# Two heads of a recurrence on opposite halves of the partitions, with PSUM tiles of their own

## The chip, the cores and the metric

The kernel runs on one core of a Trainium2 chip. The metric is the device time of the core in microseconds. The median of three runs of the kernel before is 3598.74 us (3598.61 to 3620.54).

## The reference

Two layers of a decoder trunk run on a prompt of 1024 positions and on 8 samples of 4 positions, at width 1024. One projection of the normalised input feeds two branches: a linear recurrence of 8 heads (RWKV-7) and a sliding-window attention. Their outputs are gated and merged, and a convolutional feed-forward block follows. All inputs are float32. The change concerns the recurrence, which per head keeps a 64x64 state:

```
def step(S, inp):
    r_t, w_t, k_t, v_t, kk_t, a_t = inp
    sk = jnp.einsum('bhvk,bhk->bhv', S, kk_t)
    S = (S * w_t[:, :, None, :]
         - sk[..., None] * (kk_t * a_t)[:, :, None, :]
         + v_t[..., None] * k_t[:, :, None, :])
    return S, jnp.einsum('bhvk,bhk->bhv', S, r_t)
S_T, y = lax.scan(step, wkv0, (r, w, k, v, kk, a))
```

## The kernel before

**Stages.** A layer first projects its input and prepares the operands of the recurrence (`rw_proj`, `rw_elem`), then runs the recurrence, then attention, merge and feed-forward. The loop over positions is replaced by chunks of 64 positions, 16 chunks in all; two chunks are a segment, so there are 8 segments a layer. The 8 heads stand in 4 pairs (`hp`), and in a pair head h=0 uses partitions 0 to 63 of the operands and h=1 partitions 64 to 127 (`hs[h]`).

**A segment.** `rw_elem` computes psL (L532) per head, already in the stage before. `m_front` loads BK, RA and VV, computes psG (L575; two halves q, per half four matmuls for each head, evicted by VectorE into GB), scales BK on GpSimd (L580), transposes it to psT (L585), which ScalarE copies to Bt (L586), and transposes VV to psV (L589), which ScalarE copies to the upper half of UV (L591). `m_inv` inverts the 32x32 blocks by 62 VectorE operations and a trip through HBM into Tt. `m_comb` joins two 32x32 blocks to one of 64 by three groups of 16 matmuls or transposes of 32x32 (L628, L631, L634) with a ScalarE copy behind each.

**A chunk.** `m_chain` does the dependent steps for each chunk c. x: `xb` collects GB·UV for each head (L658) and RA·S for each pair (L663 to L665), where the state S of a pair is a block-diagonal 128x128. VectorE copies the upper half to X (L670). u: `ub` gets Tt·X per head (L673), and ScalarE writes its negative to the lower half of UV (L674). sb: Bt·UV per head (L677), added on VectorE to the decayed state SW (L683; SW comes from GpSimd, L669). y: GB·UV into the lower half of `xb` (L685), copied by ScalarE to Y (L688). `m_post` normalises Y and transposes it (psY, L820); `m_sample` does the same recurrence for the samples in small pieces (psS L760, psSn L786).

**Fill.** Behind the steps, `fill` issues matmuls of an independent projection (psg, L373 to L375, float32r, 352 columns), from a generator that goes on in later stages. HK says how many portions go behind each step of a chunk. A portion is two groups of three matmuls.

**Order and pools.** The order of the instructions on each engine is made by a scheduler that looks at dependencies and at free buffers; only the place of the fill is pinned (behind the last matmul of a step). PSUM has 8 banks: one for fill (`pd`), four for psG, psT, psV, comb, psY and the samples (`pg`, tag g), and three for the chain (xb, ub, sb).

Attention, in a later stage, has one place that the prediction looks at: psQ, where for eight sequences the program issues a matmul with 128 moving columns (L891) and one with 32 (L892) in turn, each pair on the next of four column quarters.

Of the kernel before, what the change touches and what calls it, by code (L numbers as in the profile page):

```python
# [60 lines left out]
KC = {}  # L61
# [67 lines left out]
class Trunk:  # L129
# [299 lines left out]
    def rw_elem(self, l, hp, sg, zz):  # L429
# [97 lines left out]
        gm = self.cst("gmask", 64, p=64, o=64).unsqueeze(1).to_broadcast([64, 4, 64])  # L527
        for h in range(2):
            hs = slice(64 * h, 64 * h + 64)
            ps = self.pg.tile([64, 4, 64], F32, name="psL", tag="g")  # L530
            for c in range(4):
                self.lastL = nc.tensor.matmul(ps[:, c, :], BK[hs, 128 * c:128 * c + 64], RA[hs, 128 * c + 64:128 * c + 128], start=True, stop=True)  # L532
            V.tensor_tensor(Lm[:, :, h, :], ps, gm, ALU.mult)
# [12 lines left out]
    def m_state(self):  # L546
        nc, rw = self.nc, self.rw
        self.st = [rw.tile([128, 4, 128], F32, name=f"st{i}") for i in range(2)]
        self.X = rw.tile([128, 4, 128], F32, name="X")
        for t in self.st:  # L550
            nc.gpsimd.memset(t, 0.0)

    def m_front(self, l, sg):
# [13 lines left out]
        gm = self.cst("gmask", 128).unsqueeze(1).to_broadcast([128, 4, 128])  # L567
        for q in range(2):
            for h in range(2):
                hs = slice(64 * h, 64 * h + 64)  # L570
                ps = self.pg.tile([128, 4, 128], F32, name="psG", tag="g")
                for i in range(4):
                    hp, c = 2 * q + i // 2, i % 2
                    cs = slice(128 * c, 128 * c + 128)
                    nc.tensor.matmul(ps[:, i, :], BK[hs, hp, cs], RA[hs, hp, cs], start=True, stop=True)  # L575
                V.tensor_tensor(GB[:, 2 * q:2 * q + 2, :, h, :].rearrange("p a c t -> p (a c) t"), ps, gm, ALU.mult)
# [4 lines left out]
        for q in range(2):  # L581
            pt = self.pg.tile([128, 4, 128], F32, name="psT", tag="g")
            for i in range(4):
                hp, c = 2 * q + i // 2, i % 2
                nc.tensor.transpose(pt[:, i, :], BW[:, hp, c], ident)  # L585
            A.copy(Bt[:, 2 * q:2 * q + 2].rearrange("p a c t -> p (a c) t"), pt)  # L586
# [3 lines left out]
        for c in range(2):  # L590
            A.copy(UV[64:128, :, c, :], pv[64 * c:64 * c + 64])  # L591
        return dict(RA=RA, GB=GB, Bt=Bt, UV=UV)

    def m_inv(self, l, sg):
# [19 lines left out]
        for b in range(2):  # L614
            q[IQ[1]].dma_start(Tt[64 + 32 * b:96 + 32 * b, :, 32 * b:32 * b + 32],
                              rd[:, 16 * b:16 * b + 16])
        return Tt

    def m_comb(self, l, sg, m, Tt):
        nc, rw = self.nc, self.rw  # L620
        A, GB = nc.scalar, m["GB"]
        m["Tt"] = Tt
        TB = rw.tile([128, 16, 32], F32, name="TB", tag="TB")
        G = GB.rearrange("p a c h t -> p (a c h) t")
        pt = self.pg.tile([128, 16, 32], F32, name="psT1", tag="g")
        p1, p2, p3 = pt[0:32], pt[96:128], pt[64:96]
        for u in range(16):
            nc.tensor.transpose(p1[:, u, :], Tt[64:96, u, 0:32], self.con[64:96, KC["ident"] + 64:KC["ident"] + 96])  # L628
        A.copy(TB[0:32], p1)
        for u in range(16):  # L630
            nc.tensor.matmul(p2[:, u, :], G[0:32, u, 96:128], TB[0:32, u, :], start=True, stop=True)  # L631
        A.copy(TB[96:128], p2)
        for u in range(16):
            nc.tensor.matmul(p3[:, u, :], TB[96:128, u, :], Tt[96:128, u, 32:64], start=True, stop=True)  # L634
        A.activation(Tt[64:96, :, 32:64], p3, AF.Copy, scale=-1.0)

    def m_chain(self, l, sg, m):
# [6 lines left out]
        for c in range(2):  # L644
# [3 lines left out]
            xb = self.px.tile([128, 4, 128], F32, name="xb", tag="x", bufs=PM[2])  # L648
            ub = self.px.tile([64, 4, 128], F32, name="ub", tag="u")
            sb = self.px.tile([128, 4, 64], F32, name="sb", tag="s")  # L650
            X = self.X
            for hp, h in ph:
                last = first and hp == 3 and h == 1
                if last:
                    nc.tensor.matmul(xb[0:64, hp, hs[h]], GB[64:128, hp, c, h, 0:64], UV[64:128, hp, c, hs[h]], start=False, stop=False)
                    mm = nc.tensor.matmul(xb[64:128, hp, hs[h]], GB[64:128, hp, c, h, 64:128], UV[64:128, hp, c, hs[h]], start=False, stop=True)
                else:
                    nc.tensor.matmul(xb[:, hp, hs[h]], GB[64:128, hp, c, h, :], UV[64:128, hp, c, hs[h]],  # L658
                                     start=hp == h == 0, stop=False)
            if not first:  # L660
                r = 128 * c
                for hp in range(3):
                    nc.tensor.matmul(xb[:, hp, :], RA[:, hp, r:r + 128], S0[:, hp, :], start=False, stop=False)  # L663
                nc.tensor.matmul(xb[64:128, 3, :], RA[:, 3, r + 64:r + 128], S0[:, 3, :], start=False, stop=True)
                mm = nc.tensor.matmul(xb[0:64, 3, :], RA[:, 3, r:r + 64], S0[:, 3, :], start=False, stop=False)  # L665
            if not first:
                SW = rw.tile([128, 4, 64], F32, name="SW", tag="SW")
                for h in range(2):
                    P.tensor_tensor(SW[hs[h]], S0[hs[h], :, hs[h]], self.wc[hs[h], :, n:n + 1].to_broadcast([64, 4, 64]), ALU.mult)  # L669
            V.tensor_copy(X[64:128], xb[64:128])  # L670
            self.fill(HK[0], mm)
            for hp, h in ph:
                mm = nc.tensor.matmul(ub[:, hp, hs[h]], Tt[64:128, 4 * hp + 2 * c + h, :], X[64:128, hp, hs[h]], start=True, stop=True)  # L673
            A.activation(UV[0:64, :, c, :], ub, AF.Copy, scale=-1.0)  # L674
            self.fill(HK[1], mm)
            for hp, h in ph:
                mm = nc.tensor.matmul(sb[hs[h], hp, :], Bt[:, hp, c, hs[h]], UV[:, hp, c, hs[h]], start=True, stop=True)  # L677
            for h in range(2):
                s1 = S1[hs[h], :, hs[h]]
                if first:  # L680
                    V.tensor_copy(s1, sb[hs[h]])
                else:
                    V.tensor_tensor(s1, sb[hs[h]], SW[hs[h]], ALU.add)  # L683
            for hp, h in ph:
                mm = nc.tensor.matmul(xb[0:64, hp, hs[h]], GB[0:64, hp, c, h, 0:64], UV[0:64, hp, c, hs[h]],  # L685
                                 start=False, stop=hp == 3 and h == 1)
            self.lastM = mm
            A.copy(Y[64 * c:64 * c + 64], xb[0:64])  # L688
            self.fill(HK[2], mm)
        if sg == 7:  # L690
            for h in range(2):
                nc.sync.dma_start(self.a["o_pwkv"][l, :, 64 * h:64 * h + 64, :].rearrange("a k v -> k a v"), S1[hs[h], :, hs[h]])
# [51 lines left out]
    def m_sample(self, l, S):  # L744
# [6 lines left out]
        X = self.X[0:64]  # L751
# [419 lines left out]
    def run(self):  # L1171
# [42 lines left out]
        for l in range(self.layers):  # L1214
# [8 lines left out]
            self.tt = [self.iv.tile([128, 16, 64], F32, name=f"Tt{i}") for i in range(2)]  # L1223
# [165 lines left out]
```

## Time and profile before

| | |
|---|---|
| median of three runs | 3598.74 us |
| profiled execution, first to last instruction | 3583.3 us |
| TensorE busy | 3505.3 us, 98% |
| VectorE, ScalarE, GpSimd busy | 56%, 30%, 25% |
| DMA, mean busy share of the queue's engines | 30.7% |
| recurrence of layer 0, from 300 to 615 us | 302.56 of 315 us TensorE busy, granted clock 0.91 |
| recurrence of layer 1, from 2069 to 2412 us | 331.45 of 343 us TensorE busy, granted clock 0.88 |

The profile is one execution on the chip. The span runs from the first to the last instruction. A matmul of float32 operands appears as two passes, one of float32r operands or a transpose as one. The ends of matmuls are modelled and overlap the start of what follows, so the cost of a stretch of matmuls is the time from its first start to the first start behind it. "64*64" behind a matmul is the part of the array it uses (rows that are contracted, by columns). Of the granted clock, 1.00 is 2.4 GHz and 0.50 is 1.2 GHz.

### The profile page before, as it was taken

The page shows a single profiled execution, that of the slowest core. Times are in us where ns is not written, and L with a number is a line of the kernel's source. Part 1 is how long each engine was busy: PE and PEld are TensorE (multiplying, and loading weights), DVE is VectorE, ACT ScalarE, POOL GpSimd, SP SyncE. Part 2 cuts the span into 40 slices and gives each one's busy share as a digit, 9 for nine tenths or more (in the row PEclk, how much of TensorE's full clock was granted, in tenths as well). Part 3 has the DMA queues.
Part 4 walks back from the last instruction along what each step waited for, and adds up shares of the span by engine and source line. Part 5 has one row for each costly group of instructions (what it writes and reads, how often), then busy time and mean ns, then how long its engine had stood idle before and what let it go on. Part 6 is the DMA issues. An engine that isn't in the chain of part 4 may idle for free. (4 is left out here: it accounts for less than half of the span.)

```text
span 3583.3 us, 60195 instructions
## 1 busy us (share of the span) xinstructions
PE 3505.3 (98%) x24022; PEld 3316.4 (93%) x24022; DVE 2019.3 (56%) x4177; ACT 1081.4 (30%) x1854; POOL 879.5 (25%) x1070
## 2 busy tenths in 40 slices
PE   8999999999999999999999999999999999999998
PEld 7998887888999999999999988878889999999998
DVE  5767775564545445445557767746644544544445
ACT  4442222354331222112334422223533212212222
POOL 5541122131221111111346312212212211111112
PEclk9999998999999999999999989889999999999999
DMA  3345442525531111111223444325265311111111
GB/s 124 103 125 151 114 108 78 190 73 184 194 127 49 42 48 49 40 48 49 69 93 114 129 126 123 98 73 192 73 206 176 115 43 48 49 46 42 48 39 69
DMA packets 268920, 346.32 MB, mean 97 GB/s; under 512 B 82064, under 2 KB 213136, under 8 KB 268352
## 3 DMA queue, kind: packets, MB, share of 16 engines
q1 hardware_dynamic: 267488, 342.21, 30.7%
q8 instruction: 189, 3.10, 0.4%
q14 instruction: 91, 0.75, 0.1%
q10 hardware_dynamic: 1152, 0.26, 0.0%
HBM read 246.16 MB, written 98.25 MB: 96 GB/s over the span
## 5 line engine op out<-in xcount | busy, mean ns | idle before, releaser
L223 PE MATMUL psd<-lo,wh 128*128 128x352 f32 (+1 forms) x4368 | 1413.5, 324 | 3.9 <-DVE lo L244 3.9
L222 PE MATMUL psd<-hi,wh 128*128 128x352 f32 (+1 forms) x4368 | 1401.5, 326 | 11.0 <-DVE z L280 4.6
L224 PE MATMUL psd<-hi,wl 128*128 128x352 f32 (+1 forms) x4368 | 1405.8, 324 | 0.0
L222 PEld LDWEIGHTS psd<-hi,wh 128*128 128x128 f32 x4368 | 819.0, 188 | 16.4 <-ACT hi L243 4.1
L223 PEld LDWEIGHTS psd<-lo,wh 128*128 128x128 f32 x4368 | 824.8, 189 | 7.8 <-DVE lo L244 5.9
L224 PEld LDWEIGHTS psd<-hi,wl 128*128 128x128 f32 x4368 | 821.2, 188 | 1.9 <-DVE lo L244 0.2
L214 ACT CAST wh<-wr 128x1024 fp32r<-128x1024 f32 (+2 forms) x364 | 269.5, 742 | 1232.9 <-PE psd L223 894.5
L373 PE MATMUL psg<-hi,wh 128*128 128x352 f32 x1056 | 373.1, 353 | 24.5 <-DVE gt L379 22.7
L374 PE MATMUL psg<-lo,wh 128*128 128x352 f32 x1056 | 355.3, 336 | 0.0
L375 PE MATMUL psg<-hi,wl 128*128 128x352 f32 x1056 | 355.0, 336 | 0.0
L1105 DVE TENSOR_TENSOR xa<-xa,psd 128x352 f32<-128x352 f32 x456 | 226.9, 518 | 122.6 <-PE psd L224 111.2
L280 DVE TENSOR_TENSOR cz<-psd,rs 128x352 f32<-128x352 f32 (+2 forms) x176 | 72.1, 431 | 340.3 <-PE psd L224 339.7
L1078 POOL COPY cpo<-cz 128x2 f32<-128x2 f32 x44 | 8.1, 185 | 1024.4 <-DVE cz L280 1024.4
L215 DVE TENSOR_TENSOR wl<-wr,wh 128x256 fp32r<-128x256 f32 (+2 forms) x293 | 224.0, 767 | 55.6 <-ACT wh L214 55.3
L373 PEld LDWEIGHTS psg<-hi,wh 128*128 128x128 f32 x1056 | 207.5, 196 | 46.0 <-DVE gt L379 27.8
L375 PEld LDWEIGHTS psg<-hi,wl 128*128 128x128 f32 x1056 | 207.4, 196 | 5.1 <-issue 3.4
L374 PEld LDWEIGHTS psg<-lo,wh 128*128 128x128 f32 x1056 | 208.5, 197 | 2.3 <-issue 0.5
L1086 DVE SCALAR_TENSOR_TENSOR ct<-cz,prm,ct 128x1024 f32<-128x1024 f32 x88 | 159.1, 1808 | 62.8 <-ACT ct L1083 60.2
L215 POOL TENSOR_TENSOR wl<-wr,wh 128x1024 fp32r<-128x1024 f32 x71 | 171.3, 2413 | 39.8 <-ACT wh L214 38.3
L1093 DVE TENSOR_TENSOR ct<-psd,ct 128x352 f32<-128x352 f32 x132 | 64.9, 521 | 192.0 <-POOL ct L1089 154.7
L608 DVE TENSOR_TENSOR it<-R,Lt 128x60 f32<-128x60 f32 (+24 forms) x496 | 133.9, 270 | 26.6 <-POOL R L603 13.5
L610 DVE TENSOR_TENSOR R<-R,it 128x60 f32<-128x60 f32 (+24 forms) x496 | 129.9, 262 | 12.0
(314 smaller groups left out, 4511.0 us busy)
## 6 DMA issues: line engine op xcount, KB each, us to landing
wr<-wff SPq DMA_DIRECT2D x88, 512.0 KB
wr<-win SPq DMA_DIRECT2D x72, 512.0 KB
wr<-wdn SPq DMA_DIRECT2D x152, 128.0 KB
td<-gt SPq DMA_DIRECT2D x96, 176.0 KB
gl<-td SPq DMA_DIRECT2D x32, 528.0 KB
ox<-od SPq DMA_DIRECT2D x16, 528.0 KB
rt<-td SPq DMA_DIRECT2D x48, 176.0 KB
td<-rt SPq DMA_DIRECT2D x48, 176.0 KB
```

Source lines behind the costliest of these rows:

```text
L214: nc.scalar.copy(wh, wr)
L215: (sub or nc.vector).tensor_tensor(wl, wr, wh.bitcast(F32), ALU.subtract)
L222: self.nc.tensor.matmul(ps, wh, xh[:, s], start=i == 0, stop=False)
L223: self.nc.tensor.matmul(ps, wh, xl[:, s], start=False, stop=False)
L224: self.nc.tensor.matmul(ps, wl, xh[:, s], start=False, stop=i == last)
L373: nc.tensor.matmul(ps, wh[:, k], hi[:, s], start=k == 0, stop=False)
L374: nc.tensor.matmul(ps, wh[:, k], lo[:, s], start=False, stop=False)
L375: nc.tensor.matmul(ps, wl[:, k], hi[:, s], start=False, stop=k == 7)
L608: V.tensor_tensor(tv, R[:, 0:c, j:j + 1].to_broadcast([128, c, i]), Lt[:, j:j + 1, j + 1:32].to_broadcast([128, c, i]), ALU.mult)
L610: V.tensor_tensor(R[:, 0:c, j + 1:32], R[:, 0:c, j + 1:32], tv, ALU.subtract)
L1086: V.scalar_tensor_tensor(t[:, 0:TP], z[:, i:i + TP], w[i], t[:, 0:TP], ALU.mult, ALU.add)
L1105: V.tensor_tensor(x[:, s], x[:, s], ps, ALU.add)
```

## The change

The second head of each pair is mirrored: for h=0 V and X and T stand in partitions 64 to 127 and U in 0 to 63, as before; for h=1 it is the other way round. So the two heads of a pair contract over different halves of the array's rows. Each head has a PSUM tile of its own, and the program writes the matmuls of the two heads alternately.

- psL: one PSUM tile per head, heads alternate.
- psG: each 128-column matmul becomes two of 64 columns, so that h=1 lands mirrored; twice as many matmuls, on four positions of the array.
- Bt, UV: ScalarE's copies are cut by head, 3 for Bt per half instead of 1, 4 for UV per segment instead of 2.
- comb: one PSUM tile, one TB and three ScalarE operations for each head.
- m_chain: xb and ub become one tile per head, x and u side by side in one bank; the state is 128x4x64 instead of block-diagonal 128x4x128; RA·S is 16 matmuls of 64x64 for a chunk instead of 5 for whole pairs; X copies, the negation of u and the copy of Y are done per head; the state's addition and SW are one operation instead of two.
- Tt is loaded by 4 DMAs a segment instead of 2; the memset of the states goes.

The core of the diff:

```diff
+        psL = [self.pg.tile([64, 4, 64], F32, name=f"psL{h}", tag="g") for h in range(2)]
+        for c in range(4):
+            for h in range(2):
+                self.lastL = nc.tensor.matmul(psL[h][:, c, :], BK[hs[h], 128 * c:128 * c + 64],
+                                              RA[hs[h], 128 * c + 64:128 * c + 128], start=True, stop=True)
         for h in range(2):
-            for c in range(4):
-                self.lastL = nc.tensor.matmul(ps[:, c, :], BK[hs, 128 * c:128 * c + 64], RA[hs, 128 * c + 64:128 * c + 128], start=True, stop=True)
...
         for q in range(2):
+            ps = [self.pg.tile([128, 4, 128], F32, name=f"psG{h}", tag="g") for h in range(2)]
+            for i in range(4):
+                hp, c = 2 * q + i // 2, i % 2
+                for e in range(2):
+                    cs = slice(128 * c + 64 * e, 128 * c + 64 * e + 64)
+                    for h in range(2):
+                        nc.tensor.matmul(ps[h][hs[h ^ e], i, :], BK[hs[h], hp, cs], RA[hs[h], hp, 128 * c:128 * c + 128],
+                                         start=True, stop=True)
...
-            A.copy(Bt[:, 2 * q:2 * q + 2].rearrange("p a c t -> p (a c) t"), pt)
+            bt = Bt[:, 2 * q:2 * q + 2].rearrange("p a c t -> p (a c) t")
+            A.copy(bt[:, :, hs[0]], pt[:, :, hs[0]])
+            for e in range(2):
+                A.copy(bt[hs[1 - e], :, hs[1]], pt[hs[e], :, hs[1]])
...
         for c in range(2):
-            A.copy(UV[64:128, :, c, :], pv[64 * c:64 * c + 64])
+            for h in range(2):
+                A.copy(UV[hs[1 - h], :, c, hs[h]], pv[hs[c], :, hs[h]])
...
+            xu = [self.px.tile([128, 2, 4, 64], F32, name=f"xb{h}", tag=f"x{h}", bufs=PM[2]) for h in range(2)]
...
+                        mm = nc.tensor.matmul(xu[h][:, 0, hp, :], GB[k, hp, c, h, :], UV[k, hp, c, hs[h]],
+                                              start=hp == 0, stop=False)
             if not first:
                 r = 128 * c
-                for hp in range(3):
-                    nc.tensor.matmul(xb[:, hp, :], RA[:, hp, r:r + 128], S0[:, hp, :], start=False, stop=False)
...
+                for hp in range(4):
+                    for e in range(2):
+                        for h in range(2):
+                            mm = nc.tensor.matmul(xu[h][hs[h ^ e], 0, hp, :], RA[hs[h], hp, r + 64 * e:r + 64 * e + 64],
+                                                  S0[hs[h], hp, :], start=False, stop=e == 1 and hp == 3)
...
-            A.activation(UV[0:64, :, c, :], ub, AF.Copy, scale=-1.0)
+            for h in range(2):
+                A.activation(UV[hs[h], :, c, hs[h]], xu[h][hs[1 - h], 1], AF.Copy, scale=-1.0)
```

The scheduler puts the new operations into an order of its own. These are TensorE's rows at the front of segment 3 of layer 0 (psT is Bt's transpose, psV that of V, L648 the first part of comb, xb the two heads' x, st the state). In the kernel before, where the same front ends the fill:

```order
L585 MATMUL psT<-con,BK 128x128 x4
L589 MATMUL psV<-con,VV 128x128 x4
L673 MATMUL ub<-X,Tt_368 64x64 x8
L373 MATMUL psg<-hi,wh 128x352
L374 MATMUL psg<-lo,wh 128x352
L375 MATMUL psg<-hi,wl 128x352
L373 MATMUL psg<-hi,wh 128x352
L374 MATMUL psg<-lo,wh 128x352
L375 MATMUL psg<-hi,wl 128x352
L677 MATMUL sb<-UV,Bt 64x64 x8
L685 MATMUL xb<-UV,GB 64x64 x8
```

And in the changed kernel:

```order
L594 MATMUL psT<-con,BK 128x128 x8
L601 MATMUL psV<-con,VV 128x128 x4
L648 MATMUL psT_5461<-con,Tt_368 32x32 x8
L648 MATMUL psT_5490<-con,Tt_368 32x32 x8
L679 MATMUL xb_5562<-UV,GB 128x64 x4
L686 MATMUL xb_5562<-st_3900,RA 64x64 x8
L679 MATMUL xb_5563<-UV,GB 128x64 x4
L686 MATMUL xb_5563<-st_3900,RA 64x64
L651 MATMUL psT_5461<-TB,GB 32x32 x8
L651 MATMUL psT_5490<-TB,GB 32x32 x8
L686 MATMUL xb_5563<-st_3900,RA 64x64 x7
```

The transposes moved from between the steps of the previous chunk to the front of the next one: comb's first part and then L679, which reads the UV that psV fills, stand right behind them, and the x of one head (xb_5562) with its RA·S stands whole ahead of the other's.

On ScalarE, at the same place, the kernel before copies Bt and UV in four operations, two steps of the chain ahead of the comb's copy TB:

```order
L586 COPY Bt<-psT 128x512 x2
L591 COPY UV<-psV 64x4x128 x2
L674 ACTIVATE UV<-ub 64x4x128
L214 CAST wh<-wr 128x1024
L688 COPY Y<-xb 64x512
L807 ACTIVATE gsq<-Y 128x512
L629 COPY TB<-psT_5284 32x512
```

and the changed kernel:

```order
L712 COPY Y<-xb_5172 64x4x64
L712 COPY Y<-xb_5173 64x4x64
L596 COPY Bt<-psT 128x4x64
L598 COPY Bt<-psT 64x4x64 x2
L831 ACTIVATE gsq<-Y 128x512
L596 COPY Bt<-psT 128x4x64
L598 COPY Bt<-psT 64x4x64 x2
L604 COPY UV<-psV 64x4x64 x4
L649 COPY TB<-psT_5461 32x256
```

The four copies have become ten, they stand behind both copies of Y, and gsq (a square for the normalisation of Y) has come in between.

## Rows read from the trace of the kernel before

**Rows 1.** Section 1 of the page: busy time, share of span, instructions of each engine.

```profile
PE 3505.3 (98%) x24022; PEld 3316.4 (93%) x24022; DVE 2019.3 (56%) x4177; ACT 1081.4 (30%) x1854; POOL 879.5 (25%) x1070
```

**Rows 2.** Windows of both recurrences: us; busy us of each engine; granted clock; DMA.

```profile
300.00:615.00 315.00, 302.56 (x2801) 257.74 (x2800) 220.78 (x642) 80.58 (x143) 64.11 (x74) 0.91 0.41 111
2069.00:2412.00 343.00, 331.45 (x2951) 283.24 (x2949) 225.96 (x643) 85.02 (x150) 69.60 (x77) 0.88 0.38 103
```

**Rows 3.** Waits of TensorE in the whole run: us in total, times, longest us.

```profile
PE psT L628 <- DMA Tt<-rd: 2.5, 2, 1.7
PE psY L820 <- ACT UV L591: 2.0, 2, 1.0
```

**Rows 4.** Timeline of TensorE, layer 0: start us, modelled us, operation, passes.

```profile
458.51 0.61 PE L663 MATMUL xb<-st,RA 128*128 128x128 f32 x4
459.41 0.43 PE L373 MATMUL psg<-hi,wh 128*128 128x352 f32 x1
462.40 1.14 PE L673 MATMUL ub<-X,Tt 64*64 64x64 f32 x16
463.48 0.43 PE L373 MATMUL psg<-hi,wh 128*128 128x352 f32 x1
464.63 0.69 PE L677 MATMUL sb<-UV,Bt 128*64 128x64 f32 x16
465.25 1.14 PE L685 MATMUL xb<-UV,GB 64*64 64x64 f32 x16
```

**Rows 5.** The same timeline at psL, psS, and psQ of attention.

```profile
286.79 0.96 PE L532 MATMUL psL<-RA,BK 64*64 64x64 f32 x16
...
480.52 1.08 PE L760 MATMUL psS<-s,RAs 64*64 64x256 f32 x8
...
806.11 0.44 PE L891 MATMUL psQ<-az,Qs 64*32 64x128 f32 x8
806.35 0.25 PE L892 MATMUL psQ<-kr,Qs 64*32 64x32 f32 x7
806.84 0.43 PE L396 MATMUL psr<-lo,wh 128*128 128x352 f32 x1
```

**Rows 6.** The same timeline at the front of a segment, with idle before and releaser.

```profile
547.89 1.71 PE L575 MATMUL psG<-RA,BK 64*128 64x128 f32 x16
549.53 0.66 PE L585 MATMUL psT<-con,BK 128*128 128x128 f32 x4
550.78 0.66 PE L585 MATMUL psT<-con,BK 128*128 128x128 f32 x4 [0.60 <-POOL BK L580]
551.27 0.60 PE L589 MATMUL psV<-con,VV 128*128 128x128 f32 x4
553.43 0.33 PE L820 MATMUL psY<-con,Y 128*128 128x128 f32 x1 [0.98 <-ACT UV L591]
554.68 2.00 PE L658 MATMUL xb<-UV,GB 64*128 64x64 f32 x16
556.61 0.94 PE L663 MATMUL xb<-st,RA 128*128 128x128 f32 x6
557.47 1.74 PE L631 MATMUL psT<-TB,GB 32*32 32x32 f32 x32
```

**Rows 7.** ScalarE by line and shape: busy us, mean ns of one, idle before.

```profile
L586 ACT COPY Bt<-psT 128x512 f32<-128x512 f32 x32 | 18.7, 583 | 138.4 <-PE psT L585 138.4
L688 ACT COPY Y<-xb 64x512 f32<-64x512 f32 x32 | 18.5, 579 | 55.3 <-PE xb L685 36.9 <-DVE st L683 17.7 <-POOL SW L669 0.8
L807 ACT ACTIVATE gsq<-Y 128x512 f32<-128x512 f32 x16 | 10.1, 629 | 19.7 <-DVE R L610 13.6 <-DVE Y L806 5.8
L998 ACT COPY pT<-psP 128x256 f32<-128x256 f32 x8 | 2.9, 365 | 4.1 <-PE psP L996 4.1
```

**Rows 8.** The 13 windows in which the granted clock was half: the longest, the sum.

```profile
557.80:581.70 23.90, 23.90 (x124) 15.83 (x121) 8.49 (x28) 3.12 (x6) 4.61 (x4) 0.50 0.20 62
sum 139.80, PE 138.34 PEld 110.80 DVE 64.48 ACT 14.32 POOL 13.83; mean PE 10.64 PEld 8.52 DVE 4.96 ACT 1.10 POOL 1.06
```

## What the change is expected to do to the time

> **What bounds the kernel now.** I read the page first: TensorE is busy 98% of the span [rows 1]. Then the windows of the two stages that the change touches, the recurrences of layer 0 and layer 1: in 315 and 343 us TensorE is busy all but 12 us each, VectorE about two thirds, ScalarE and GpSimd a quarter or less, and the clock granted to TensorE averages 0.91 and 0.88 [rows 2]. The waits of TensorE say the same: those on work that the change touches are 2.5 us (comb's psT for the load of Tt) and 2.0 (psY, a transpose, for ScalarE's copies into UV) in the whole run [rows 3]. So in these stages a stretch of matmuls costs what the timeline shows from its first start to the start of the next stretch, and every wait that the change adds to TensorE counts in full.
>
> **Prices from the timeline.** The profile lists passes: an f32 matmul is two. u, 16 passes of 64 columns all on one 64x64 position, takes 462.40 to 463.48, 1.07 us. sb, 16 passes alternating between two column halves, takes 464.63 to 465.25, 0.62 [rows 4]. Two unknowns, two rows: 16p+s=1.07 and 8p+s=0.62 give p=0.056 a pass and s=0.17 for the change of array shape; I use 0.058 and 0.15. Row halves: psS sends 8 passes of 256 columns to alternating row halves with PSUM tiles of their own, 1.08 modelled, about 1.01 to the next start [rows 5]; on one position 8 passes of four times 0.056 would take 1.8. So row halves overlap as column halves do, if the two PSUM tiles differ. All column quarters at once: psQ's 32 passes (16 of 128, 16 of 32 columns) lie between 806.11 and 806.84 [rows 5], against 16×0.11+16×0.03=2.2 in a row. Two row halves times two column halves, as the change makes of psG and RA·S, stand in no row.
>
> **The stream, term by term (both layers, 32 chunks, 16 segments).**
> - u: 32×(1.07−0.62) = −14.
> - psL: 16 passes in 0.96 modelled, 0.89 to the next start [rows 5], 32 times; alternating 0.61. −9.
> - y: as u (465.25 row, 1.14 modelled). About half of the first chunks keep the heads in blocks (below), so 17 chunks gain: −7.5.
> - x (L658): 1.93 from 554.68 to 556.61 [rows 6], 0.11 a pass. In 13 of 32 chunks the heads alternate: 8×0.11+0.15=1.05, −11.4. In 18 the new order puts one head, then RA·S, then the other: one more shape change, +0.2 each. −8.
> - RA·S: 0.90 for four of its five matmuls (458.51 to 459.41, [rows 4]), with the fifth at a quarter more some 1.2 a chunk. Now 32 passes on four positions: 8×0.058+0.15=0.6 where heads alternate (13 chunks), twice 0.6 where not. −8 if four positions run at once, −2 if two; I take −5.
> - psG: 1.64 for 16 passes [rows 6], 3.28 a segment. Now 64 passes of 0.11: 2.1 if spread evenly over four positions in two pieces, 3.8 if they overlap in pairs. The order sends them unevenly and in more pieces; I take 3.0, about the middle. −4 (bounds −19 and +8).
> - comb: 32x32 pieces, 32 passes of L631 in 1.67 of 1.74 modelled [rows 6]. Heads stay in blocks of 8; psG's row shows that a block's start overlaps the end of the one before by about 0.25. L631 and L634: −5.
> - Against: psS, which overlapped well, is broken up where comb now holds two of the four pg tiles (both passes of one head, then comb, then the other head): +3. More pieces of fill between small stretches: +3.
> Sum −46. Some 140 of the 658 us run at half clock [rows 2, 8] and so hold a ninth of the work, which costs twice: −50.
>
> The Trainium skill, "TensorE: Matmul & The Clock Gate", Part 3, says matmuls start and end strictly in program order; psQ's rows disagree: the program alternates L891 and L892, yet eight passes of L891, on four positions, start ahead of the first of L892 [rows 5]. By it four positions would not refill freely and psG would lie nearer its upper bound, +12 on the sum. "TensorEngine Tiling (Array Packing)", Key Properties, has a change of mode drain the array; that speaks against more pieces, and the 0.15 above agrees.
>
> **What the change adds.** ScalarE: Bt goes from one copy to three per half segment, UV from two to four, u and Y from one to two each. The 128x512 copy takes 583 ns, a 128x256 one 365 [rows 7]; a 64x256 copy has no row, so it lies between half of 579, 0.29, and 0.58; I take 0.365, the row with the same columns. That is harmless where fill covers it: after u there is 1.15 us of fill (463.48 to 464.63, [rows 4]) against 2×0.365+0.2. It is not harmless at the front of a segment. There the new order has psT x8, psV x4, L648 x16 and then at once L679, which reads UV. TensorE's part is 0.49 (550.78 to 551.27) + 1.67 (550.78 to 553.43 less the 0.98 idle) = 2.16. ScalarE starts at psT's modelled end, 0.66, and needs six Bt copies and the first UV copy: 0.66+7×0.365=3.2. Wait 1.05. With gsq between them (0.63) 1.7; with psY first, which needs all four UV copies, 1.1 more. By the order, segments 2 to 7 are such fronts: 0.95+1.7+1.7+2.4+2.3+1.4 = 10.4 a layer. The same place costs 1.0 to 1.3 a layer before [rows 6]. So +18 in both (bounds: +13 at 0.29 a copy, +33 at 0.58). GpSimd's Bt scaling (the 0.60 at 550.78) comes behind a shorter psG in more fronts: +3. VectorE's X copy becomes two and its state add one; GpSimd loses one SW each chunk; both engines have room [rows 2]. Two more small loads of Tt on the sync queue: psT waits 2.5 in all for them [rows 3], left at that.
>
> **Half clock.** 140 us of the two stages are at 0.50 (last row of [rows 8]), and the longest stretch, 557.80 to 581.70, follows the psY wait and the small matmuls of the front without fill [rows 6]. New waits sit at just such places in 12 fronts. I add 10: one more stretch as long as that costs half its 24 us.
>
> **Sum.** −50+18+3+10 = −19. The profiled span is 3583.3, and 15.4 lie around it to the median of 3598.7 (the three runs: 3598.6, 3598.7, 3620.5). Span 3564, time 3580.
>
> **Rivals.**
> - Waits hidden. If fills or the release of UV copy by copy cover the front, and the shorter stream leaves half clock as it is: −50+6 = 3555. For: VectorE and ScalarE have long idle times [rows 2]. Against: the printed order has no fill there.
> - Only pairs overlap. psG +12, RA·S +3, u, y and x as above: 3595. For: no row of two row halves by two column halves. Against: psQ.
> - Row halves don't overlap in these shapes (64 columns): u, y, x, psL lose 38: 3618. Against: psS.
> - Slower, by the clock. If each front with its wait drops TensorE to half clock as at 557.80, twelve fronts instead of the two that do now: ten stretches at half of 24 us are up to 120 more; half of them make +60, 3640. It decides from five further such stretches, +60, on. For: psY's wait of 1 us and what follows it [rows 6, 8]. Against: the other stretches now, which make up the sum of 140, are mostly far shorter than the one at 557.80.
> - No effect: not possible for u, whose order alternates everywhere.
>
> **How the numbers follow.** The sum 0.43 (own range 3562 to 3605), waits hidden 0.22, only pairs 0.12, the clock 0.18, row halves 0.05. About 1%, 36 us, is what a measurement of this kernel can tell from no change: faster means under 3563, slower over 3635. Faster 0.24 (hidden and a little of the sum), within 0.60, slower 0.16 (nearly all of the clock's). Range 3548 to 3640, which leaves out the lower edge of hidden and the upper half of the clock.
>
> **What would show it.** Right: u's 16 passes in about 0.6; psG's stretches between 1.0 and 1.5 per 32 passes; a wait of 1 to 2.5 us before L679 or psY for ScalarE's UV copies in six fronts a layer; 130 to 160 us at half clock. Wrong: u still at 1.07 (row halves), psG near 3.8 a segment (pairs), no idle before L679 (hidden), or 200 us and more at half clock.

## The result, and the profile after

The changed kernel is slower: 3641.11 us median of six runs (3633.53 to 3645.80), against 3612.44 for six runs of the kernel before beside them. The ratio is 1.0078, with a 95% interval of 1.0055 to 1.0101. I had forecast 3580 and a range up to 3640, with the sign the other way. Run again later beside other kernels, it came to 1.0071 (1.0047 to 1.0095):

> The changed kernel itself beside these variants on one chip: 3633 to 3646, 0.5 to 1.0% above the kernel before.

The profiled execution has a span of 3636.8 us, 53.5 more than that of before. The page's first section, its row of the granted clock in 40 slices, and the view by cores (span, mean granted clock):

```profile
PE 3526.9 (97%) x25198; PEld 3307.8 (91%) x25198; DVE 1993.6 (55%) x4177; ACT 1122.4 (31%) x2062; POOL 858.1 (24%) x1040
PEclk9999777999999999999999997769999999999999
core 0: 3636.8 us, clock 0.951
```

TensorE is busy 97% and still the bound [rows 1]. What changed is the clock: 0.951 on average against 0.973 before. The loss sits in the two recurrences. Windows of about the same stretches as in [rows 2]:

```profile
300.00:655.00 355.00, 329.90 (x3445) 270.84 (x3446) 206.65 (x643) 101.61 (x248) 55.86 (x62) 0.80 0.36 100
2095.00:2440.00 345.00, 320.38 (x3353) 258.89 (x3351) 206.29 (x632) 101.17 (x246) 53.40 (x60) 0.78 0.36 100
```

0.80 and 0.78, where [rows 2] has 0.91 and 0.88.

To see where 53.5 us come from, I split TensorE's time in each trace into three parts, which add up to the span less some 17 us that lie before its first matmul and behind its last: the idle time before instructions; the time from each matmul's start to the next one's, less that idle, with the parts that lie in stretches at half clock counted half (the **stream**, the work at full clock); and the other half of those parts (**lost at half clock**). Before: 3416 stream, 89 lost, 61 idle. After: 3359, 168, 93. So the change gains 57 in the stream, and loses 79 by the clock and 32 by waiting. One thing makes the measured difference of runs (29) smaller than that of the two profiles (53): the profiled execution of before was a good one. Its mean clock was 0.973, and that of 56 further runs of the same kernel was 0.960 to 0.971. So 79 overstates what the clock costs. Reckoned from the span and the mean clock of every run, as span × (1 − clock), the repeated runs of the changed kernel lose 181 us on average and the runs of before beside them 126: the clock costs some 55. With the 57 gained and the 32 waited this gives +30, where the runs show +29 and +27.

**The stream did what the change says.** Timeline of TensorE after (L532 is psL, L695 u, L577 psG, L701 sb, L708 y), the rows that answer to [rows 4] and [rows 5]:

```profile
285.70 0.68 PE L532 MATMUL psL<-RA,BK 64*64 64x64 f32 x16
286.31 0.41 PE L222 MATMUL psl<-wah,w2a2h 64*128 64x288 f32 x2
...
513.67 0.68 PE L695 MATMUL xb<-X,Tt 64*64 64x64 f32 x16
514.28 0.43 PE L373 MATMUL psg<-hi,wh 128*128 128x352 f32 x1
515.45 0.87 PE L577 MATMUL psG<-RA,BK 64*64 64x128 f32 x20
516.25 0.68 PE L701 MATMUL sb<-UV,Bt 128*64 128x64 f32 x14
...
519.95 0.68 PE L708 MATMUL xb<-UV,GB 64*64 64x64 f32 x16
520.56 0.43 PE L373 MATMUL psg<-hi,wh 128*128 128x352 f32 x1
```

psL's 16 passes take 0.61 (0.89 before), u's 0.61 (1.07), y's 0.61. These are good places: the mean over all chunks, at full clock, is 0.78 for u and 0.85 for y, as some are cut into pieces by other work. 20 passes of psG take 0.80, or 0.033 each beyond 0.15 for the change of shape. One position needs 0.11 for such a pass, so between three and four of the four positions run at once; the first four passes start within 0.02 us of each other. The Trainium skill, "TensorE: Matmul & The Clock Gate", Part 3, has matmuls start strictly in program order. As with psQ, the trace fits free positions better than pairs.

**The waits.** TensorE's waits in the whole run, the rows that answer to [rows 3]:

```profile
PE psg L373 <- DVE gt L379: 26.2, 23, 2.6
PE xb L679 <- ACT UV L604: 14.6, 9, 3.5
PE psT L594 <- POOL BK L589: 7.4, 8, 1.9
PE psT L594 <- DVE R L623: 6.7, 2, 3.8
PE psn L1231 <- POOL sq L1228: 11.0, 3, 5.0
```

14.6 us of x waiting for ScalarE's copies into UV are nearly all new (before, UV cost 2.3 in all), and so are nearly all of the 7.4 for GpSimd's scaling of BK and the 6.7 for VectorE's inversion. The last row is not in the recurrence at all: it lies in the first 40 us of the kernel, at the sums of squares of the input (psn), where the scheduler now puts GpSimd's work in another order than before.

**The clock.** One front of a segment after (L594 psT, L601 psV, L844 psY, L679 x, L686 RA·S), the rows that answer to [rows 6], and the window at half clock that begins in it, with the sum over six such windows of layer 0:

```profile
522.68 0.87 PE L577 MATMUL psG<-RA,BK 64*64 64x128 f32 x20
523.49 0.66 PE L594 MATMUL psT<-con,BK 128*128 128x128 f32 x4
525.12 0.66 PE L594 MATMUL psT<-con,BK 128*128 128x128 f32 x4 [0.97 <-POOL BK L589]
526.33 0.66 PE L601 MATMUL psV<-con,VV 128*128 128x128 f32 x4 [0.55 <-DVE GB L585]
...
528.74 0.30 PE L844 MATMUL psY<-con,Y 128*128 128x128 f32 x1 [0.68 <-ACT UV L604]
528.97 1.45 PE L679 MATMUL xb<-UV,GB 64*128 64x64 f32 x8
530.35 1.12 PE L686 MATMUL xb<-st,RA 64*64 64x64 f32 x16
```
```profile
529.60:550.00 20.40, 20.40 (x178) 17.38 (x177) 10.24 (x39) 5.58 (x14) 2.56 (x2) 0.50 0.15 39
sum 122.80, PE 122.69 PEld 96.34 DVE 44.83 ACT 28.39 POOL 12.54; mean PE 20.45 PEld 16.06 DVE 7.47 ACT 4.73 POOL 2.09
```

From 522.68 to 540.46 there is no fill, and the clock is at half from 529.6 to 550.0. RA·S of one head (L686, 16 passes) then takes 1.04, where the prices of before put it at 0.61 at full clock. Half clock stretches the work without fill itself, so the fill behind it comes later. Before, one such stretch in layer 0 and three in layer 1 were longer than 10 us; after, six and seven are, one in nearly every segment. The one that [rows 8] show is the longest of layer 0 alone. Two of layer 1:

```profile
2284.90:2302.00 17.10, 17.10 (x143) 15.39 (x142) 7.11 (x25) 3.61 (x7) 0.00 (x0) 0.50 0.04 13
2332.70:2360.00 27.30, 27.30 (x144) 19.27 (x144) 10.78 (x36) 3.13 (x6) 5.31 (x5) 0.50 0.17 52
```

### The profile page after: what moved, and what is told of

Its sections match the earlier page's. It is cut to its first block, busy times and chain, and to the rows that moved or that the text cites. A ratio compares the mean times of both kernels' runs of the same rounds, so it can differ in the third digit from the quotient of the medians.

```text
span 3636.8 us, 62832 instructions
## 1 busy us (share of the span) xinstructions
PE 3526.9 (97%) x25198; PEld 3307.8 (91%) x25198; DVE 1993.6 (55%) x4177; ACT 1122.4 (31%) x2062; POOL 858.1 (24%) x1040
## 5 line engine op out<-in xcount | busy, mean ns | idle before, releaser
L222 PEld LDWEIGHTS psd<-hi,wh 128*128 128x128 f32 x4368 | 817.9, 188 | 13.6 <-ACT hi L243 5.0
L373 PE MATMUL psg<-hi,wh 128*128 128x352 f32 x1056 | 382.5, 362 | 26.2 <-DVE gt L379 26.2
L374 PE MATMUL psg<-lo,wh 128*128 128x352 f32 x1056 | 362.7, 343 | 0.0
L621 DVE TENSOR_TENSOR it<-R,Lt 128x60 f32<-128x60 f32 (+24 forms) x496 | 118.6, 239 | 42.8 <-POOL R L616 22.8
L623 DVE TENSOR_TENSOR R<-R,it 128x60 f32<-128x60 f32 (+24 forms) x496 | 120.2, 242 | 12.9
```

Of the source, the lines that this page charges most:

```text
L222: self.nc.tensor.matmul(ps, wh, xh[:, s], start=i == 0, stop=False)
L373: nc.tensor.matmul(ps, wh[:, k], hi[:, s], start=k == 0, stop=False)
L374: nc.tensor.matmul(ps, wh[:, k], lo[:, s], start=False, stop=False)
L621: V.tensor_tensor(tv, R[:, 0:c, j:j + 1].to_broadcast([128, c, i]), Lt[:, j:j + 1, j + 1:32].to_broadcast([128, c, i]), ALU.mult)
L623: V.tensor_tensor(R[:, 0:c, j + 1:32], R[:, 0:c, j + 1:32], tv, ALU.subtract)
```

## The experiments

Three theories of the lost clock. W: idle waits at a segment's front make it fall. N: the front is a stretch of small matmuls with too little fill, waits or not. D: the packed matmuls themselves, shorter and on parts of the array, are what it falls on. Stream, lost and idle are of one profiled execution each, split as above, in us; the medians of before are those of the sets of runs beside which the variants ran. The lost time of one profile is a single draw, and that of before is a low one. So the last column has span × (1 − clock), the mean over all runs of the variant, less that of the runs of before beside them, in us.

| run | ratio to before (95%) | median us | stream | lost | idle | clock, all runs |
|---|---|---|---|---|---|---|
| before | | 3609.5 to 3615.3 | 3416 | 89 | 61 | 0 |
| after | 1.0078 (1.0055 to 1.0101) | 3641.1 | 3359 | 168 | 93 | not on record |
| after, the same again | 1.0071 (1.0047 to 1.0095) | 3636.8 | 3358 | 173 | 92 | +55 |
| e1_uv_first | 0.9999 (0.9978 to 1.0021) | 3616.5 | 3363 | 159 | 79 | +36 |
| e2_front_fill | 0.9819 (0.9772 to 0.9867) | 3548.2 | 3353 | 85 | 90 | −29 |
| e2b, the same again | 0.9841 (0.9814 to 0.9868) | 3555.0 | 3354 | 92 | 86 | −13 |
| e13_split_fill | 0.9823 (0.9791 to 0.9854) | 3550.8 | 3354 | 91 | 84 | −22 |
| e9_two_R | 0.9872 (0.9825 to 0.9920) | 3563.2 | 3352 | 109 | 87 | −6 |
| e10_comb_fill | 0.9893 (0.9850 to 0.9936) | 3569.0 | 3355 | 94 | 103 | −18 |
| e6_early_front | 0.9894 (0.9844 to 0.9945) | 3579.5 | 3353 | 118 | 86 | +1 |
| e12_early_x_fill | 0.9712 (0.9686 to 0.9739) | 3510.2 | 3360 | 66 | 68 | −56 |
| e12b, the same again | 0.9719 (0.9692 to 0.9746) | 3511.1 | 3360 | 70 | 67 | −51 |
| e5_before_front | 1.0106 (1.0044 to 1.0168) | 3648.7 | 3411 | 137 | 72 | +33 |
| e3_before_split | 0.9957 (0.9932 to 0.9981) | 3589.5 | 3418 | 99 | 53 | −14 |
| e7_before_fill | 0.9959 (0.9924 to 0.9994) | 3592.0 | 3420 | 74 | 64 | −22 |
| e14_before_early | 0.9892 (0.9861 to 0.9923) | 3576.9 | 3421 | 60 | 61 | −41 |

### The waits for UV taken away: e1_uv_first

```diff
+        pv = self.pg.tile([128, 4, 128], F32, name="psV", tag="g")
+        for hp in range(4):
+            nc.tensor.transpose(pv[:, hp, :], VV[:, hp, :], ident)
+        for c in range(2):
+            for h in range(2):
+                A.copy(UV[hs[1 - h], :, c, hs[h]], pv[hs[c], :, hs[h]])
         for q in range(2):
             ps = [self.pg.tile([128, 4, 128], F32, name=f"psG{h}", tag="g") for h in range(2)]
...
```

(The same lines go from their old place behind psT.)

> The changed kernel with V's transposes (psV) and ScalarE's copies of them into UV written ahead of psG instead of behind psT, so that x no longer waits behind Bt's six copies; the rest as it is. In the changed kernel the two stages' small matmuls cost 57 us less than before at full clock, idle of TensorE is 32 us more, and half clock costs 78 us more (167 against 89). Theory W (the idle waits at a segment's front make the granted clock fall): the wait of L679's counterpart for ScalarE's UV copies (14.6 us) goes, and half clock goes back towards before's: it costs 90 to 120 us, time 3565 to 3600. Theory N (the front is a long stretch of small matmuls without fill, waits or not): the waits go, but half clock still costs 150 or more, time 3610 to 3635.

No wait for UV is left before x. A front in its timeline (L600 psT, L679 x), and the window at half clock that begins in it:

```profile
533.52 0.66 PE L600 MATMUL psT<-con,BK 128*128 128x128 f32 x4
534.10 0.66 PE L679 MATMUL xb<-UV,GB 64*128 64x64 f32 x8
536.16 0.66 PE L679 MATMUL xb<-UV,GB 64*128 64x64 f32 x4 [1.40 <-DVE GB L591]
...
540.18 0.66 PE L373 MATMUL psg<-hi,wh 128*128 128x352 f32 x1
```
```profile
538.80:562.70 23.90, 23.90 (x211) 21.07 (x211) 15.97 (x54) 6.52 (x17) 3.61 (x4) 0.50 0.29 75
```

159 us are still lost at half clock, 9 fewer than in the changed kernel, and idle is 14 less; the time came back to that of before. By all runs the clock costs 36 more than before, where the changed kernel's costs 55 more, so a part of the loss did go with these waits. Theory W gave 90 to 120 lost; as the main cause it falls here. N's range for the time (3610 to 3635) holds 3616.5. The front still has transposes, x, RA·S and comb in a row without fill up to 540.18, and the clock falls within it. But this run took away one wait, not all: the front shown waits 1.40 us for VectorE's GB instead. That waits are not needed for the fall, the trace of e6 shows below.

### The fill moved to the front: e2_front_fill, and again

```diff
-            self.fill(HK[2], mm)
+            if c == 0 or sg == 7:
+                self.fill(HK[2], mm)
...
                     ms.append(self.m_front(l, sg + 1))
+                    self.fill(HK[2], self.pvm)
```

(`pvm` is the last transpose of psV.)

> The changed kernel with the two portions of fill that follow a segment's last y moved behind psV's transposes, between them and comb's first part; no other fill is added. Theories W and N: the fill covers ScalarE's copies and splits the stretch, so the waits for UV all but go (under 3 us) and half clock costs 90 to 120 us: 3560 to 3600. Theory D (the packed small matmuls themselves, being over sooner and on parts of the array, are what the clock falls on, wherever the fill stands): waits go, half clock still costs 150 or more: 3610 to 3630.

> The same kernel as in the run e2_front_fill, a second time beside the others: 3540 to 3560 if that result holds, 3580 or more if it was a lucky day of the clock.

In the program two portions of fill change places with the transposes, nothing else. A front in its timeline, from the last transpose to the next fill:

```profile
503.76 0.27 PE L601 MATMUL psV<-con,VV 128*128 128x128 f32 x1
503.79 0.41 PE L373 MATMUL psg<-hi,wh 128*128 128x352 f32 x1
...
505.88 0.54 PE L648 MATMUL psT<-con,Tt 32*32 32x32 f32 x16
506.36 1.24 PE L679 MATMUL xb<-UV,GB 64*128 64x64 f32 x16
507.53 0.44 PE L686 MATMUL xb<-st,RA 64*64 64x64 f32 x10
...
509.71 0.43 PE L373 MATMUL psg<-hi,wh 128*128 128x352 f32 x1
```

Two things follow. The scheduler now keeps the heads together: x's 16 passes take 1.17 instead of two pieces. And 85 us are lost at half clock, half of the changed kernel's 168, with the same packed matmuls (stream 3353); by all runs the clock now costs less than in before, where the changed kernel's costs 55 more. D falls. W and N gave the same ranges for this run, so it does not tell them apart. It does show that the idle time as a whole is not what counts: idle is 90, as in the changed kernel (93), since the waits for UV went and others came (fill waits 40 us for VectorE to evict psg, 26 after), and still the clock is back. The kernel is 1.8% faster than before, 2.6% faster than the changed kernel. The second time gave 0.9841, the same within the intervals.

### The same front given to the kernel before: e5_before_front

```diff
+    def behind(self, sg):
+        return self.tc.issue_after(self.lastM.ins) if sg > 1 else nullcontext()
...
-                nc.tensor.transpose(pt[:, i, :], BW[:, hp, c], ident)
+                with self.behind(sg):
+                    nc.tensor.transpose(pt[:, i, :], BW[:, hp, c], ident)
...
```

(The transposes of psV alike.)

> The kernel before with the transposes of the next segment (psT, psV) held behind the last y of the segment, which puts them at the front as the scheduler does in the changed kernel; matmuls and copies are those of before. Theory N: the front without fill makes the clock fall here too, half clock costs 120 or more against 89, and with 5 to 12 us of waits the time is 3640 to 3680 where before is 3600 to 3612. Theory W: in between, as one copy per transposed tile makes shorter waits: 3620 to 3640. Theory D: only the waits, up to +12.

Matmuls and copies are those of before, only the transposes stand at the front. A front in its timeline (L590 psT, L634 comb, L664 x), and the window at half clock that begins in it:

```profile
535.54 0.60 PE L590 MATMUL psT<-con,BK 128*128 128x128 f32 x4
...
536.50 0.64 PE L634 MATMUL psT<-con,Tt 32*32 32x32 f32 x16
538.01 2.00 PE L664 MATMUL xb<-UV,GB 64*128 64x64 f32 x16 [0.87 <-ACT UV L597]
...
541.42 0.66 PE L374 MATMUL psg<-hi,wh 128*128 128x352 f32 x1
```
```profile
540.70:561.20 20.50, 20.50 (x158) 17.07 (x157) 6.58 (x24) 3.66 (x7) 0.40 (x1) 0.50 0.11 23
```

48 us more are lost at half clock than in the profile of before, 33 more by all runs, and idle is 11 more; 1.0106 against before. So the order of the front makes the clock fall in the old kernel too, without any of the change's matmuls. The time lies in N's range (3640 to 3680), above W's (3620 to 3640); with waits at these fronts as well, such as the 0.87 for UV above, it does not rule W out by itself.

### The front written earlier, and the fill behind x: e6_early_front, e12_early_x_fill

```diff
-                Y = self.m_chain(l, sg, ms[sg])
-                if sg < 7:
-                    ms.append(self.m_front(l, sg + 1))
+                nxt = (lambda: ms.append(self.m_front(l, sg + 1))) if sg < 7 else None
+                Y = self.m_chain(l, sg, ms[sg], nxt)
```

(`m_chain` runs `nxt` between its two chunks.)

> The changed kernel with the next segment's front (psG, psT, psV and their copies) written between the two chunks of a segment instead of behind both; in the order of TensorE the transposes now stand behind RA.S of the second chunk, comb's first parts beside u, and the heads alternate in x, RA.S and y. Theories W and N: no wait for UV, shorter stretches without fill, half clock 80 to 110 us, stream 60 to 70 us below before: 3530 to 3570. Theory D: half clock stays at 150 or more: 3590 to 3620.

e6 lost 118 us at half clock and came to 3579.5, between the ranges of N (to 110, to 3570) and of D (from 150, from 3590). By its order the transposes had left the front, but comb's parts, x and RA·S still stood in a row there. One of its fronts, from the last fill on, and the window at half clock that begins in it:

```profile
548.38 0.32 PE L375 MATMUL psg<-hi,wl 128*128 128x352 f32 x1
548.63 0.54 PE L648 MATMUL psT<-con,Tt 32*32 32x32 f32 x16
549.10 1.10 PE L681 MATMUL xb<-UV,GB 64*128 64x64 f32 x8
...
551.68 1.71 PE L651 MATMUL psT<-TB,GB 32*32 32x32 f32 x32
```
```profile
551.70:596.10 44.40, 44.40 (x312) 31.88 (x311) 10.93 (x22) 8.27 (x23) 9.37 (x9) 0.50 0.18 52
```

TensorE waits for nothing here, and none of Bt's or V's transposes (L594, L601) stands in the row. None of e6's eight windows at half clock above 10 us has a wait of TensorE in the 7 us ahead of it. So neither waits nor those transposes are needed for the clock to fall, and W falls as the whole cause. In the changed kernel, though, all thirteen such windows have a wait in the 7 us ahead; whether waits add to the fall or lengthen it, no run separates.

e12 cuts the row of e6 too:

```diff
+            if c == 0 and sg:
+                self.fill(HK[2], mm)
             if not first:
                 r = 128 * c
...
-            self.fill(HK[2], mm)
+            if c == 0 or sg == 7:
+                self.fill(HK[2], mm)
```

(At the first place `mm` is the last matmul of x.)

> The run e6_early_front (the next segment's front written between the two chunks) with the two portions of fill behind a segment's last y moved behind x of the next segment's first chunk, ahead of RA.S. By the order no stretch between two portions of fill at the front of a segment then holds more than comb's two parts and x. Theory N: half clock costs 60 to 85 us (118 in e6_early_front), stream as there, waits 75 to 90: 3520 to 3550, below e2_front_fill. If half clock comes with the packed shapes after all (theory D): 100 or more, 3560 to 3580.

> The kernel of the run e12_early_x_fill again, beside the kernel before with the same placement: 3500 to 3520 if that result holds.

e12 is the fastest kernel of the study, 0.9712 and again 0.9719 (0.9692 to 0.9746). A segment's front in its timeline (L681 x, L690 RA·S), with fill at four places, and the windows of both recurrences:

```profile
457.32 0.43 PE L373 MATMUL psg<-hi,wh 128*128 128x352 f32 x1
...
459.51 1.11 PE L681 MATMUL xb<-UV,GB 64*128 64x64 f32 x16
460.55 0.43 PE L373 MATMUL psg<-hi,wh 128*128 128x352 f32 x1
...
462.44 0.32 PE L373 MATMUL psg<-hi,wh 128*128 128x352 f32 x1
...
463.49 0.69 PE L690 MATMUL xb<-st,RA 64*64 64x64 f32 x32
464.11 0.43 PE L373 MATMUL psg<-hi,wh 128*128 128x352 f32 x1
```
```profile
300.00:615.00 315.00, 299.22 (x3595) 251.04 (x3594) 217.17 (x652) 106.69 (x257) 55.19 (x62) 0.92 0.41 115
2044.00:2358.00 314.00, 299.87 (x3588) 251.00 (x3586) 216.62 (x648) 108.11 (x259) 55.68 (x62) 0.92 0.40 111
```

RA·S of both heads, 32 passes on four positions, takes 0.62, half of before's mean of 1.2. The clock is 0.92 in both stages. Since e6 differs from it only in the place of two portions of fill, e6's miss is a matter of that place, not of D.

### How much is the placement, how much the matmuls: e14_before_early, e7_before_fill

The two edits of e12 on the kernel before (e14), and the one of e2 on it (e7):

> The kernel before with the two edits of the run e12_early_x_fill: the next segment's front written between the two chunks, and the two portions of fill behind a segment's last y moved behind x of the next segment's first chunk. If placement alone gives what e12 has: 3510 to 3530. If the mirrored matmuls keep their gain of the stream (56 us at full clock) once the clock is out of the way: half clock 60 to 80 us, stream 3416 as in before, 3560 to 3585.

> The kernel before with the two portions of fill that follow a segment's last y moved behind psV's transposes, the same edit as in the run e2_front_fill. By the order only the front of segment 7 changes much, since elsewhere the transposes already stand ahead of the last y. If the shorter matmuls are what makes that run faster: 0 to 15 us below before. If the place of the fill alone does: 40 us or more below before.

e14 and e12b, run beside each other: 0.9892 and 0.9719. The placement alone is worth 1.1%, all of it by the clock (41 us by all runs, of a mean gain of 39); the mirrored heads are worth 1.7% more once the clock is out of their way (stream 3421 against 3360, which is 61 us of the 66 between the medians 3576.9 and 3511.1). e7 gained 0.4%, nearer what the shorter matmuls as the cause of e2's gain would leave to it (0 to 15 us) than what the place of the fill alone would (40 or more); most of its fronts had their transposes elsewhere already, so the edit moved the fill to a place where little needed it.

### The cut copies alone: e3_before_split

```diff
-            A.copy(UV[64:128, :, c, :], pv[64 * c:64 * c + 64])
+            for h in range(2):
+                A.copy(UV[64:128, :, c, 64 * h:64 * h + 64], pv[64 * c:64 * c + 64, :, 64 * h:64 * h + 64])
```

(Bt, u and Y alike.)

> The kernel before with ScalarE's copies of Bt, UV, u and Y cut into as many pieces as in the changed kernel; all matmuls as before. By the order the transposes still stand ahead of u or sb, not at the front. If the front without fill is what costs (theory N): ScalarE has some 38 us more work, nearly all hidden, half clock costs 80 to 110 us, time within 0.5% of before. If the cut copies cost by themselves (my forecast's term): 10 to 20 us of waits, 3620 to 3635 beside 3600 to 3615.

0.9957: twice as many copies cost nothing in the old order, which the scheduler changed a little for them. In this order, with fill between a copy and its reader, ScalarE's added work stays hidden.

### Three that gave little: e13_split_fill, e9_two_R, e10_comb_fill

> The changed kernel with one of the two portions behind a segment's last y moved behind psV, and the other behind comb's first part, ahead of x. Theory N: the front is cut in two places, half clock costs 60 to 85 us, 3525 to 3550. Theory W: the wait for UV is covered as in e2_front_fill, so the same time as there within 8 us.

e13 came out as e2 (0.9823), with 91 lost. This is what W gave for it, and N's ranges are missed. So once two portions stand at the front it does not matter that they stand apart; N in the form "the shorter each stretch the better" is not borne out here.

> The run e2_front_fill (fill behind psV) with two buffers for R, the tile of the inversion, so that its start no longer waits on GpSimd and the DMA of the one before; VectorE then starts the inversion earlier and evicts fill sooner. There psg waits 40 us for VectorE (22.7 before). If these waits and the dips of the clock behind them are worth anything: waits 20 to 30 us, half clock 70 to 85 us, 3525 to 3545. If VectorE's order sets them, not R: as e2_front_fill, 3548.

A second buffer for R left 34.5 us of waits of psg for VectorE (40.2 in e2), and the intervals of the two ratios overlap. So R is not what sets these waits. That VectorE's order sets them was the forecast's other branch; no run shows it by itself.

> The run e9_two_R with one more portion of fill behind comb's second part (16 portions in all, 14 of them taken from those behind the recurrence of each layer, so that the fill left for later stages is the same). Theory N: the rest of the stretch without fill at the front is cut again, half clock falls by 10 to 25 us against e9_two_R and so does the time: 3510 to 3535. Theory W or D: half clock stays within 8 us of e9_two_R.

One more portion behind comb's second part: 94 lost instead of 109, idle 103 instead of 87, and the same time. psT now waits 12.9 us for GpSimd (4.8 in e9) and u 8.8 for the copies of X, so what the fill saved in clock went into waits. N's forecast of the time (3510 to 3535) was wrong here.

## Why the prediction was wrong

**The sum of the stream was nearly right in size.** Forecast −46, measured −57 (3416 to 3359), term by term at full clock: u −10 (forecast −14), psL −9 (−9), y −8 (−7.5), x −9.5 (−8), RA·S −8 (−5), psG −11 (−4), comb −6 (−5), psS +2 (+3), fill +2 (+3). psG was mis-sized: four positions do run at once, 2.6 us a segment where I took 3.0. "Only pairs overlap" and "row halves don't overlap" fall.

**The waits were right in place, and as a whole too small.** Forecast +18 for ScalarE's copies at the front and +3 for GpSimd. Measured are 14.6 and 0.7 for UV, against 2.3 before, and 7.4 for GpSimd, 6.2 more; a 64x256 copy took 367 ns, as I had taken it (365). Not forecast were 6.7 us of psT waiting for VectorE's inversion, and 11.0 at the kernel's start, which every variant of the changed kernel has (10 to 13) and none of the kernel before: a by-product of the scheduler's new order that no run isolated. Idle grew by 32 in all. "Waits hidden" falls.

**The step that failed is the half clock.** I wrote "I add 10: one more stretch as long as that costs half its 24 us". It came to 79 between the two profiles, and to some 55 by the clocks of all runs. I had both pieces: the printed order put transposes, comb, x and RA·S in a row without fill, in six segments of each layer, and [rows 6, 8] show that the front of this form in layer 0 before was followed by 24 us at half clock; its like in layer 1 was followed by 27. My own rival, "Slower, by the clock", says "twelve fronts instead of the two that do now" and 3640 us; the result is 3641. The rival's count of fronts held, but that the numbers meet is in part luck: the rival meant 41 us above a median of 3598.74, and the result is 29 above one of 3612.44.

I gave the rival 0.18 because I took the other stretches at half clock before for "mostly far shorter". I had misread them. The one at 557.80 was called the longest and is not; four of the thirteen windows, of 23.9, 20.5, 17.1 and 27.3 us, hold 89 of the 140. Nine were short (3.4 to 6.8), mostly behind fronts of another form, with the transposes already done; but the one of 17.1 at 2284.9 follows such a front too, with comb, x and RA·S in a row and no wait. The count of fronts with a long row without fill was to be taken, not the average window.

A smaller misreading: the 13.6 of the 15.4 us between the profiled span and the median are not time around the span. In every later run the time is 1.8 us more than its span; the profile was of a faster execution.

I also put the fall down to the new waits ("New waits sit at just such places"). As the reason this does not hold: e1 takes the waits for UV away and 36 of the 55 us stay, and in e6 the clock falls at fronts with no wait at all.

**What stays open** is the exact condition for the fall. Stretches without fill of more than 6 us at full clock, idle included, number 2 in before's two stages, 12 in the changed kernel's, 4 in e2 and 4 or 5 in e12 (two lie at the edge), which fits; but 7 in e1, 4 in e5 and 5 in e6, which lose 159, 137 and 118, and so does not. Nor did cutting such a row further always help: e13 and e10 kept their time. What the runs show is that moving fill into the front, with the same matmuls and much the same idle time, takes the loss away (e2, e12), and that moving the transposes there in the kernel before brings a part of it (e5).

## What to carry to other kernels

Packing heads on different row halves, each with a PSUM tile of its own as here, nearly halves such stretches where the heads alternate (u 1.07 to 0.61 us), and four positions run three to four times as fast as one. But where a kernel lives between two clock levels, look at what the scheduler does with the order: a gain of 57 us of matmuls was turned into a loss because fill no longer stood between the small matmuls. Count the places in the new order that look like the ones behind which the clock falls in the old trace, price each by its window, and move fill there before judging the change.

## What the hardware showed that I had not expected

- The granted clock of one kernel differs between executions by more than the change is worth: 0.960 to 0.973 for the kernel before, 3592.8 to 3627.2 us in one set of 19 runs. A single profile is one draw of it.
- Idle of TensorE and lost clock are not tied: e2 and the changed kernel idle 90 and 93 us and lose 85 and 168.
- A ScalarE copy out of PSUM costs by its columns, not its partitions: 64x256 took 367 ns and 128x256 372, so that cutting a copy by partitions doubled the time on it:

```profile
L598 ACT COPY Bt<-psT 64x256 f32<-64x256 f32 x64 | 23.5, 367 | 0.8
L596 ACT COPY Bt<-psT 128x256 f32<-128x256 f32 x32 | 11.9, 372 | 41.8 <-PE psT L594 41.2
```
